# A branch's output projection summed by 64-row halves into separate PSUM banks

## The chip, the cores and the metric

The kernel runs on one core of a Trainium2 chip. A core has a matrix engine (TensorE, PE in the profile; its weight loads are listed as PEld), a vector engine (VectorE, DVE), a scalar engine (ScalarE, ACT), a general engine (GpSimd, POOL) and a queue engine (SyncE, SP) that starts transfers. The matrix engine multiplies a stationary operand (the "weights" of the instruction, here up to 128 rows by 128 columns) with a moving operand and adds the result into an accumulator bank in PSUM; a bank holds 128 partitions by 512 float32. The metric is the device time of one execution in microseconds, lower being better.

## The reference

Two layers, each with one combined input projection, two token mixers and one output projection. The change concerns the line with `w_pa`.

```python
for l in range(DEPTH):                      # DEPTH = 2; x is (1, 256, 1024)
    h = rmsnorm(x, norm_w[l])
    proj = h @ w_in[l]
    q_a, k_a, v_a, ab_a, z_a, q_b, k_b, v_b, z_b, gate_a, gate_b = split(proj)
    y_a = gated_delta_branch(q_a, k_a, v_a, ab_a, z_a, ...)   # (1, 256, 1024)
    y_b = diff_attention_branch(q_b, k_b, v_b, z_b, ...)      # (1, 256, 1024)
    merged = (sigmoid(gate_a) * (y_a @ w_pa[l])
              + sigmoid(gate_b) * (y_b @ w_pb[l]))
    x = x + merged @ w_out[l]
return rmsnorm(x, final_norm_w)
```

Each branch's result is 256 tokens by 1024 channels and is multiplied by a 1024 by 1024 matrix.

## The kernel before, in words

All large products are taken in a float32 format that the matrix engine reads at a rounded precision (`F32R`). To keep the accuracy, each operand is split into a high part and the remainder, the low part, and a product is summed from three terms: activation high by weight high, activation high by weight low, and activation low by weight high.

A token-major projection (`proj_tm`, lines 315 to 332) makes 512 output columns for all 256 tokens. It has one accumulator bank for each of the two token tiles (m = 0 and 1, 128 tokens each), taken by `banks2` from the pool `ps_p` of four banks. Its loop runs over the eight contraction tiles kt of 128 rows, over the two token tiles, and over the three terms (lines 324, 325 and 326). The activation is stationary, 128 rows by 128 tokens; the weight tile, 128 rows by 512 columns, moves. At the end `evac` is called for each token tile.

The weights come from `weights` (line 273 on), for two contraction tiles at a time: a load of 512 KB on SP's queue into `raw` (line 304), a cast on ACT to the high part (line 308), and a subtraction on DVE to the low part (line 310). The pools of high and low parts have two buffers each, so the cast for one pair of tiles waits until the matrix engine has finished with the pair two steps earlier.

The function `branch` (line 1213 on) calls `proj_tm` twice for a branch, once for each half i of the 1024 output columns, and its `evac_p` (line 1217) multiplies the sum, read from PSUM by DVE, with the gate. The b branch's projection (`pb`) comes before the a branch's (`pa`). After `pa`, for each column half and token tile, DVE adds the two branches (line 1286), and `split_T` turns the sum with four transposes on the matrix engine into a bank of the pool `ps_m` (line 227), copies the high part on ACT (line 234) and subtracts for the low part on DVE (line 238). The result, `mT`, is the activation of the output projection (`o`), whose first half is again a `proj_tm` and whose second half is `proj_by_tile` (line 369, and 359 for the last tile in two column halves).

The pool `ps_c` has two banks. Near this place it serves the last steps of the a branch's recurrence (`chunks(0)`, during `pb`) and later the transposes of the next layer's normalised input (`prenorm`).

Each engine works through its own queue in order. The order within a queue is set when the program is built, by a planner that estimates when each instruction could run and prefers those with higher priority (the weights' loads, casts and subtractions run under `tc.high_priority`). Some instructions are tied to others by `behind`; in `branch` and in `proj_tm` none are.

The attention scores (`scores`, line 1061) are the other place that matters here: for each head and query tile they take one product on rows 64 to 127 and one on rows 0 to 63 of the same tiles, in plain float32, into two banks.

Of the kernel before, what the change touches and what calls it, by code (L numbers as in the profile page):

```python
# [8 lines left out]
F32 = mybir.dt.float32  # L9
# [3 lines left out]
ALU = mybir.AluOpType  # L13
# [4 lines left out]
P = 128  # L18
DM = 1024
KT = DM // P  # L20
SEQ = 256
NM = SEQ // P
# [27 lines left out]
def hybrid_encoder(  # L50
# [19 lines left out]
    V, S, G, T = nc.vector, nc.scalar, nc.gpsimd, nc.tensor  # L70

    def pool(name, bufs=1, space=None):
        kw = {} if space is None else {"space": space}
        return ctx.enter_context(tc.tile_pool(name=name, bufs=bufs, **kw))
# [4 lines left out]
    work = pool("work", 2)  # L79
# [9 lines left out]
    def banks2(name):  # L89
        return [ps_p.tile([P, 512], F32, tag="p", name=f"{name}{i}") for i in range(2)]  # L90

    def banks2_c(name):
        return [ps_c.tile([P, 512], F32, tag="c", name=f"{name}{i}") for i in range(2)]
# [10 lines left out]
    mark = {}  # L104
# [210 lines left out]
    def proj_tm(act, w, c0, n, evac, nm, places=(None,) * 4, spare=(), later=None, turned=(), between=None,  # L315
                banks=None, held=None, first=(), raws={}):

        accs = (banks or banks2)(f"pp_{nm}")
        for kt, hi, lo in weights(w, c0, n, nm, places, later=later, spare=spare, turned=turned, held=held,
                                  first=first, raws=raws):  # L320
            for m in range(NM):
                ts_ = slice(m * P, (m + 1) * P)
                o = accs[m][:, :n]
                T.matmul(o, act[kt // 4][:, 0, kt % 4, ts_], hi, start=kt == 0, stop=False)  # L324
                T.matmul(o, act[kt // 4][:, 0, kt % 4, ts_], lo, start=False, stop=False)  # L325
                mark["proj"] = T.matmul(o, act[kt // 4][:, 1, kt % 4, ts_], hi, start=False,  # L326
                                        stop=kt == KT - 1).ins
                mark["done", nm, kt] = mark["proj"]
        if between:
            between()  # L330
        for m in range(NM):
            evac(m, accs[m][:, :n])

    def homes(tags, nm):

        for tag, n in tags:
            t_ = big.tile([P, n, 2, 2, 512], F32R, tag=tag, name=f"w{tag}_{nm}")
            for k in range(n):
                yield t_[:, k]
# [34 lines left out]
    def proj_fm(act, w, c0, evac, nm, turned=()):  # L374
# [15 lines left out]
                         skip_group_check=True)  # L390
        for i in range(2):
            evac(accs[i], 2 * i)

    halves = (slice(0, 64), slice(64, P))

    def silu2(dst, ps):

# [109 lines left out]
    for l in range(DEPTH):  # L507
# [6 lines left out]
        def evac_v(i):  # L514
            def evac(m, ps):
                S.copy(vb[i][:, m, :], ps)
            return evac


        places = list(homes((("A", 1), ("ktm", 1), ("vtm", 1), ("B", 2)), f"vb{l}"))  # L520

        places2 = pair(f"wvb{l}")
        places2 = [t_.rearrange("p x b t -> p x (b t)").rearrange("p x (k c) -> p x k c", k=2)
                   for t_ in places2] + [places.pop(), *homes((("vtm", 1),), f"vb{l}1")]
        if l == 0:
            opening(wl, evac_v(0), places)
# [101 lines left out]
        for kt in range(KT):  # L628
            for part in range(2):
                T.matmul(abp[0:64, :SEQ], wabr[:, kt, :], hT[kt // 4][:, part, kt % 4, :],  # L630
                         start=kt == 0 and part == 0, stop=kt == KT - 1 and part == 1)
# [3 lines left out]
        for m in range(NM):  # L635
            T.matmul(abq[:, m * 32 : (m + 1) * 32], abT[:, m * P : (m + 1) * P], id2,
                     start=True, stop=True)
# [575 lines left out]
        def branch(yT, w_, gt, nm, places=(None,) * 4):  # L1213
            for i in range(2):
                def evac_p(m, ps, i=i):
                    gs = gt[i][:, m, :]
                    V.scalar_tensor_tensor(gs, gs, 1.0, ps, ALU.add, ALU.mult)
                proj_tm(yT, w_, 512 * i, 512, evac_p, f"{nm}{i}", (None,) * 4 if i else places)

        rgb = big.tile([P, 2, 2, 512], F32, tag="p8", name=f"rgb{l}", bufs=4)  # L1220
# [24 lines left out]
        for i, m in ((0, 0), (0, 1), (1, 0), (1, 1)):  # L1245
            split_B(ybT[i], yb_sent[i, m][0], m, nw[:, 1:2], mark[f"ga{l}{i}", 2 + m])
        branch(ybT, w_pb[l], gtb, f"pb{l}")
        ch = [chunks(0), chunks(1)]

# [22 lines left out]
        for m in range(NM):  # L1272
# [5 lines left out]
            V.scalar_tensor_tensor(ro[:, m], ro[:, m], 0.5, rq[:, m], ALU.mult, ALU.mult)  # L1278
            gated(osb, za, ro, nw[:, 0:1], yaT, f"ya{l}", (m,))
        branch(yaT, w_pa[l], gta, f"pa{l}")  # L1280


# [10 lines left out]
        def evac_o(i):  # L1293
            def evac(m, ps, cs=slice(0, 512)):
# [3 lines left out]

        proj_tm(mT, w_out[l], 0, 512, evac_o(0), f"o{l}0",
                [None, None] + list(homes((("ktm", 1), ("vtm", 1)), f"o{l}0")), spare=(2, 3),  # L1300
                later={2: mark[f"pa{l}0", 3], 3: mark[f"pa{l}1", 1]},
                held={2: mark["load", f"pb{l}1", 1], 3: mark["load", f"pb{l}1", 3]})
# [9 lines left out]
        for m in range(NM if not more else 0):  # L1312
            outs.append(norm_tiles("nf", m))
            h, r, ss = outs[m]
# [5 lines left out]
        for s_, _ in enumerate(o_last):  # L1320
            if more:
                prenorm(s_, xt, wb, l + 1)
            else:

                m = min(s_, 1)
                h, r, ss = outs[m]
# [5 lines left out]
                else:  # L1332
                    cs = slice(256 * (s_ - 1), 256 * s_)
                    part = ss[:, 1:2] if s_ == 1 else small.tile([P, 1], F32, tag="xsl", name="xsl", bufs=1)
# [49 lines left out]
```

## Time and profile before

| what | value |
|---|---|
| median of two runs | 750.91 us (750.02 to 751.8) |
| span of the profiled execution | 748.5 us |
| what lies between that span and the median | 2.4 us |
| TensorE busy | 739.3 us, 99% |
| TensorE weight loads busy | 641.7 us, 86% |
| DVE busy | 586.5 us, 78% |
| ACT busy | 481.2 us, 64% |
| granted TensorE clock, mean | 0.998 |

The page of the profile gives the busy time of each engine, the chain of waits that ended last, and groups of instructions by source line. A row of a tile or line view gives the number of instructions and their shortest, median and longest duration in ns; `128*128 128x512` is the size of the stationary operand and the moving one. A row of the timeline gives the start in us, the time from the first start to the last end of the merged instructions, the engine, the line, the operation, output and inputs, and how many were merged. Products of the matrix engine overlap, so the step from one start to the next says more than a duration. What an idle engine waited for stands in brackets at the end.

### The profile page before, as it was taken

What the parts mean: (1) busy time and instruction counts of PE and PEld (TensorE: products, weight loads), DVE (VectorE), ACT (ScalarE), POOL (GpSimd) and SP (SyncE); (2) the same over time, 40 slices, a digit from 0 to 9 for tenths busy, and PEclk for the clock granted to TensorE, in tenths of its full rate; (3) what the DMA queues carried; (4) which work ended last, traced back from release to release, by engine and by line L of the source; (5) the groups of instructions that cost most, each with busy time, mean ns of one, the idle gap of its engine ahead of it and who ended that gap; (6) DMA issues with size and microseconds to landing.
All of it is one profiled execution on the core that took longest, in us unless ns stands there. A gap on an engine that the chain in (4) does not pass through costs nothing.

```text
span 748.5 us, 13917 instructions
## 1 busy us (share of the span) xinstructions
PE 739.3 (99%) x5176; PEld 641.7 (86%) x5176; DVE 586.5 (78%) x1109; ACT 481.2 (64%) x1022; POOL 139.5 (19%) x221
## 2 busy tenths in 40 slices
PE   8999999999999999999999999999999999999996
PEld 6999889987888889888889899889778888998885
DVE  8696898999985965578668779999999679537782
ACT  6757875667876576645456578555687757566552
POOL 6004110112023440100000150202110425301000
PEclk9999999999999999999999999999999999999999
DMA  8754566776667462567674466767666748335641
GB/s 260 239 170 169 170 179 198 209 211 193 208 177 186 145 184 84 171 200 247 199 232 133 128 192 180 219 176 230 195 171 195 197 133 229 95 114 201 220 141 57
DMA packets 73734, 135.46 MB, mean 181 GB/s; under 512 B 12944, under 2 KB 13921, under 8 KB 73666
## 3 DMA queue, kind: packets, MB, share of 16 engines
q1 hardware_dynamic: 64750, 113.65, 50.6%
q0 software_dynamic: 7936, 19.35, 8.7%
q10 hardware_dynamic: 980, 1.58, 0.6%
q8 instruction: 41, 0.67, 0.4%
q14 instruction: 27, 0.22, 0.1%
HBM read 125.53 MB, written 9.01 MB: 180 GB/s over the span
## 4 chain that ended last, share of the span: by engine, by line
PE 95%; ACT 2%; issue 1%; DVE 1%; DMA 1%; SPq 0%; POOLq 0%; POOL 0%; DVEq 0%; ACTq 0%
PE pp_vb L369 4%; PE pp_qk L325 4%; PE pp_qk L326 3%; PE pp_qk L324 3%; PE sc L1061 2%; PE pp_o L369 2%; PE pf_k L385 2%; PE pp_za L325 2%; PE pf_v L385 2%; PE pf_v L389 2%; PE pp_gb L324 2%; PE pp_gb L325 2%; PE pp_zb L324 2%; PE pf_q L387 2%; PE pf_k L387 2%; PE pf_v L387 2%
## 5 line engine op out<-in xcount | busy, mean ns | idle before, releaser
L325 PE MATMUL pp_qk<-lo_qk,hT 128*128 128x512 f32 x128 | 50.5, 395 | 0.3
L326 PE MATMUL pp_qk<-hi_qk,hT 128*128 128x512 f32 x128 | 50.0, 390 | 0.0
L310 DVE TENSOR_TENSOR lo_qk<-raw_qk,hi_qk 128x1024 fp32r<-128x1024 f32 x32 | 39.1, 1222 | 11.6 <-ACT hi_qk L308 11.4
L324 PE MATMUL pp_qk<-hi_qk,hT 128*128 128x512 f32 x128 | 45.1, 393 | 0.0
L308 ACT CAST hi_qk<-raw_qk 128x1024 fp32r<-128x1024 f32 x28 | 29.4, 1049 | 23.4 <-PE pp_qk L326 12.4
L1071 ACT ACTIVATE es<-sc,mx 128x256 f32<-128x256 f32 x64 | 29.6, 474 | 19.5 <-DVE mx L1069 19.5
L387 PE MATMUL pf_q<-hT,hi_q 128*128 128x256 f32 x128 | 36.1, 286 | 0.0
L385 PE MATMUL pf_k<-hT,hi_k 128*128 128x256 f32 x128 | 36.1, 287 | 0.0
L385 PE MATMUL pf_v<-hT,hi_v 128*128 128x256 f32 x128 | 35.9, 285 | 0.0
L387 PE MATMUL pf_v<-hT,hi_v 128*128 128x256 f32 x128 | 35.8, 284 | 0.0
L385 PE MATMUL pf_q<-hT,hi_q 128*128 128x256 f32 x128 | 35.8, 284 | 0.0
L387 PE MATMUL pf_k<-hT,hi_k 128*128 128x256 f32 x128 | 35.8, 284 | 0.0
L310 DVE TENSOR_TENSOR lo_pb<-raw_pb,hi_pb 128x1024 fp32r<-128x1024 f32 x16 | 19.6, 1225 | 20.5 <-ACT hi_pb L308 20.2
L389 PE MATMUL pf_q<-hT,lo_q 128*128 128x256 f32 x128 | 35.2, 288 | 0.0
L389 PE MATMUL pf_v<-hT,lo_v 128*128 128x256 f32 x128 | 34.6, 288 | 0.0
L389 PE MATMUL pf_k<-hT,lo_k 128*128 128x256 f32 x128 | 34.3, 284 | 0.0
L308 ACT CAST hi_pa<-raw_pa 128x1024 fp32r<-128x1024 f32 x16 | 16.8, 1053 | 22.3 <-PE pp_pa L326 16.1
L679 DVE SCALAR_TENSOR_TENSOR cvq<-pf_q,cw,cvq 128x254 f32<-128x254 f32 (+1 forms) x64 | 30.0, 479 | 0.9 <-ACT cvq L675 0.3
L679 DVE SCALAR_TENSOR_TENSOR cvv<-pf_v,cw,cvv 128x254 f32<-128x254 f32 (+1 forms) x64 | 30.1, 482 | 0.1
L679 DVE SCALAR_TENSOR_TENSOR cvk<-pf_k,cw,cvk 128x254 f32<-128x254 f32 (+1 forms) x64 | 29.0, 478 | 1.3 <-ACT cvk L675 0.6
L325 PEld LDWEIGHTS pp_qk<-lo_qk,hT 128*128 128x128 f32 x128 | 24.0, 188 | 6.6 <-DVE lo_qk L310 1.6
L310 DVE TENSOR_TENSOR lo_pa<-raw_pa,hi_pa 128x1024 fp32r<-128x1024 f32 x16 | 19.6, 1224 | 11.1 <-ACT hi_pa L308 11.1
(414 smaller groups left out, 2542.2 us busy)
## 6 DMA issues: line engine op xcount, KB each, us to landing
raw_qk<-in_w_in_dram SPq DMA_DIRECT2D x32, 512.0 KB, 3.8
raw_k<-in_w_in_dram SPq DMA_DIRECT2D x16, 512.0 KB, 4.7
raw_q<-in_w_in_dram SPq DMA_DIRECT2D x16, 512.0 KB, 3.7
raw_v<-in_w_in_dram SPq DMA_DIRECT2D x16, 512.0 KB, 3.8
raw_zb<-in_w_in_dram SPq DMA_DIRECT2D x16, 512.0 KB, 3.7
raw_za<-in_w_in_dram SPq DMA_DIRECT2D x16, 512.0 KB, 3.7
raw_ga<-in_w_in_dram SPq DMA_DIRECT2D x16, 512.0 KB, 4.4
raw_pb<-in_w_pb_dram SPq DMA_DIRECT2D x16, 512.0 KB, 3.8
```

The lines of the kernel that those rows point to most:

```text
L308: high = (V.tensor_copy if kp in turned else S.copy)(hi[:, :, :n], raw[:, :, :n]).ins
L310: mark[nm, kp] = high, V.tensor_tensor(lo[:, :, :n], raw[:, :, :n], hi[:, :, :n].bitcast(F32), ALU.subtract).ins
L324: T.matmul(o, act[kt // 4][:, 0, kt % 4, ts_], hi, start=kt == 0, stop=False)
L325: T.matmul(o, act[kt // 4][:, 0, kt % 4, ts_], lo, start=False, stop=False)
L326: mark["proj"] = T.matmul(o, act[kt // 4][:, 1, kt % 4, ts_], hi, start=False, stop=kt == KT - 1).ins
L369: mark["proj"] = T.matmul(o, act[kt // 4][:, pa, kt % 4, ts_], ws[kt][1 + pw], start=kt == 0 and n_ == 0, stop=kt == KT - 1 and n_ == 2).ins
L385: T.matmul(o, hi[:, cs], act[kt // 4][:, 0, kt % 4, :], start=first, stop=False, skip_group_check=True)
L387: T.matmul(o, hi[:, cs], act[kt // 4][:, 1, kt % 4, :], start=False, stop=False, skip_group_check=True)
L389: T.matmul(o, lo[:, cs], act[kt // 4][:, 0, kt % 4, :], start=False, stop=done, skip_group_check=True)
L679: V.scalar_tensor_tensor(ca[:, o0:o1], acc[:, b, o0 + sft : o1 + sft], cw[:, j, cb : cb + 1], ca[:, o0:o1], ALU.mult, ALU.add)
L1061: mm = T.matmul(sp[n][:, qt * SEQ : (qt + 1) * SEQ], qkT[h // 4][rows, 0, h % 4, qt * P : (qt + 1) * P], qkT[h // 4][rows, 1, h % 4, :], s ...
L1071: S.activation(es[:, n, qt, :], spv[:, qt, :], AF.Exp, bias=mx[:, n, qt : qt + 1], accum_out=s_all[:, h, n, qt : qt + 1])
```

## The change

The projection of the a branch no longer goes through `proj_tm` but through a new function. Every product of 128 contraction rows is replaced by two products, one on rows 0 to 63 and one on rows 64 to 127 of the same operands. The lower rows are summed into two banks of `ps_p` as before, the upper rows into two banks of `ps_c`. When both are complete, ACT copies the one sum to a tile in SBUF, DVE adds the other to it, and the evacuation reads that tile instead of PSUM. The loads, casts and subtractions of the weights are the same. The tuple `halves` is defined earlier in the file, unchanged.

```diff
+    halves = (slice(0, 64), slice(64, P))
+
+    def proj_rows(act, w, c0, evac, nm):
+        accs = [banks2(f"pp_{nm}"), banks2_c(f"pu_{nm}")]
+        for kt, hi, lo in weights(w, c0, 512, nm):
+            for m in range(NM):
+                for n_, (part, w_) in enumerate(((0, hi), (0, lo), (1, hi))):
+                    for r in range(2):
+                        mark["proj"] = T.matmul(accs[r][m], act[kt // 4][halves[r], part, kt % 4, m * P : m * P + P],
+                                                w_[halves[r]], start=kt == 0 and n_ == 0,
+                                                stop=kt == KT - 1 and n_ == 2).ins
+        for m in range(NM):
+            both = work.tile([P, 512], F32, tag="w2c", name=f"sum_{nm}{m}", bufs=3)
+            S.copy(both, accs[0][m])
+            V.tensor_tensor(both, accs[1][m], both, ALU.add)
+            evac(m, both)
...
                 def evac_p(m, ps, i=i):
                     gs = gt[i][:, m, :]
                     V.scalar_tensor_tensor(gs, gs, 1.0, ps, ALU.add, ALU.mult)
+                if nm[:2] == "pa":
+                    proj_rows(yT, w_, 512 * i, evac_p, f"{nm}{i}")
+                    continue
                 proj_tm(yT, w_, 512 * i, 512, evac_p, f"{nm}{i}", (None,) * 4 if i else places)
```

More of the change, by code (lines that the diff above doesn't have):

```diff
@@ L392, in proj_fm @@
             evac(accs[i], 2 * i)
-    halves = (slice(0, 64), slice(64, P))
     def silu2(dst, ps):
```

## The prediction, made before the changed kernel ran

> **What bounds the kernel now.** The page comes first, for the engine that carries the span.
>
> ```profile
> span 748.5 us, 13917 instructions
> ...
> PE 739.3 (99%) x5176; PEld 641.7 (86%) x5176; DVE 586.5 (78%) x1109; ACT 481.2 (64%) x1022; POOL 139.5 (19%) x221
> ...
> PEclk9999999999999999999999999999999999999999
> ...
> PE 95%; ACT 2%; issue 1%; DVE 1%; DMA 1%; SPq 0%; POOLq 0%; POOL 0%; DVEq 0%; ACTq 0%
> ```
>
> TensorE (PE) is busy for 99% of the span and makes up 95% of the chain of waits; its granted clock shows no throttling in any slice. So whatever the edit adds to the PE queue, as work or as a wait, is added to the time, and whatever it adds to ACT (64% busy) or DVE (78%) costs only where PE then waits for it. The profiled execution has a span of 748.5 us against a median of 750.91: about 2.4 us lie around the span or between executions. I work out a difference from this one execution and add it to the median.
>
> The tile view of the accumulators that the edit replaces says how much work is concerned.
>
> ```profile
> L324 PE MATMUL pp_pa<-hi_pa,yaT x64: 389/389/393, 330.0 to 718.0; 128*128 128x512 f32 x64
> ...
> L325 PE MATMUL pp_pa<-lo_pa,yaT x64: 389/389/476, 330.5 to 718.2; 128*128 128x512 f32 x64
> ...
> L326 PE MATMUL pp_pa<-hi_pa,yaT x64: 389/389/395, 330.7 to 718.4; 128*128 128x512 f32 x64
> L1217 DVE SCALAR_TENSOR_TENSOR ga<-ga,pp_pa x8: 680/680/683, 340.6 to 719.0; 128x512 f32<-128x512 f32 x8
> ```
>
> There are 192 products over both layers (two layers, two column halves, eight contraction tiles, two token tiles, three terms) and 8 evacuations. The durations of 389 ns are latencies; products overlap, so the price of one is the step between starts. That needs the timeline, here at the seam between the first column half (pa0) and the second (pa1) of layer 0.
>
> ```profile
> 340.00 0.39 PE L326 MATMUL pp_pa<-hi_pa,yaT 128*128 128x512 f32 x1
> ...
> 340.23 0.39 PE L324 MATMUL pp_pa<-hi_pa,yaT 128*128 128x512 f32 x1
> 340.23 0.19 PEld L325 LDWEIGHTS pp_pa<-lo_pa,yaT 128*128 128x128 f32 x1
> ...
> 340.62 1.28 DVE L1217 SCALAR_TENSOR_TENSOR ga<-ga,pp_pa 128x512 f32<-128x512 f32 x2
> 340.68 0.39 PE L326 MATMUL pp_pa<-hi_pa,yaT 128*128 128x512 f32 x1
> ...
> 340.91 0.61 PE L324 MATMUL pp_pa<-hi_pa,yaT 128*128 128x512 f32 x2
> 341.11 1.06 ACT L308 CAST hi_pa<-raw_pa 128x1024 fp32r<-128x1024 f32 x1 [1.67 <-PE pp_pa L326]
> ...
> 344.09 1.03 PE L227 MATMUL pt_mg<-ident,ga 128*128 128x128 f32 x8
> ```
>
> Products start every 0.227 us (340.68 to 340.91), each with the next one's weights loading beside it (the load that starts at 340.23 together with a product). PE goes from pa0 to pa1 without a gap, because pa1 uses two other banks of the pool of four.
>
> **The split products: do two halves cost one whole?** Each 128-row product becomes two 64-row products, one on the lower and one on the upper rows. The nearest rows are the attention scores, which already alternate the two row halves; the windows are cut so that the pairs show.
>
> ```profile
> L1061 PE MATMUL sc<-qkT x128: 376/376/481, 165.0 to 591.0; 64*128 64x256 f32 x128
> ...
> 164.65 0.39 PE L326 MATMUL pp_zb<-hi_zb,hT 128*128 128x512 f32 x1
> ...
> 164.97 0.70 PE L1061 MATMUL sc<-qkT 64*128 64x256 f32 x4
> ...
> 165.28 0.38 PE L1061 MATMUL sc<-qkT 64*128 64x256 f32 x2
> ...
> 165.29 0.19 PEld L1061 LDWEIGHTS sc<-qkT 64*128 64x128 f32 x2
> ...
> 165.50 0.60 PE L1061 MATMUL sc<-qkT 64*128 64x256 f32 x4
> ...
> 165.72 0.38 PE L1061 MATMUL sc<-qkT 64*128 64x256 f32 x2
> ...
> 166.03 0.66 PE L608 MATMUL qkt<-ident,stg 128*128 128x128 f32 x4
> ...
> 192.42 1.14 PE L1061 MATMUL sc<-qkT 64*128 64x256 f32 x8
> 193.48 0.50 PE L325 MATMUL pp_za<-lo_za,hT 128*128 128x512 f32 x1
> 193.82 0.39 PE L326 MATMUL pp_za<-hi_za,hT 128*128 128x512 f32 x1
> ```
>
> At 165.72 two products together take 0.38 us, while one alone has a duration of 376 ns: they run side by side. So do their weight loads (165.29: two in 0.19). Pairs start every 0.22 us (165.28, 165.50, 165.72). So the new 192 pairs should cost about what 192 products cost now, 0.22 to 0.227 us each.
>
> Which one? The scores are plain float32, which streams 256 columns in about the time that the projection's format streams 512. Two rows of the projection's own format show what lies on top of the streaming.
>
> ```profile
> 735.90 1.60 PE L359 MATMUL pp_o<-wkq_o,mT 128*128 128x256 f32 x12
> ...
> 22.63 1.99 PE L630 MATMUL abp<-hT,wabr 128*64 128x256 f32 x16
> L630 PE MATMUL abp<-hT,wabr x32: 276/277/355, 22.6 to 390.6; 128*64 128x256 f32 x32
> ```
>
> With 128 weight columns the step for 256 columns is (1.60-0.28)/11 = 0.120 us (the last one's latency taken from the last row); twice the columns give 0.227, so a column costs 0.107/256 us and 0.013 us are constant. With 64 weight columns the step is (1.99-0.28)/15 = 0.114, a constant of 0.007. The constant goes with the number of weight columns loaded, and each half still loads 128. I therefore take 0.227 for a pair: 0 us. The ends are 0.22 (the scores), 192 x -0.007 = -1.3 us, and the constant paid twice, 192 x 0.013 = +2.5 us. The Trainium skill (TensorEngine Tiling (Array Packing), Performance Considerations, When to Use Tiling) recommends row tiling where the contraction is at most 64; here it is 128 and fills the array. By that rule the rate gains nothing, by the scores' row it gains the 1.3 us; no row here has this format with 64 rows.
>
> **Switching between 128 and 64 rows.** From the last whole product at 164.65 to the first pair at 164.97 is 0.32 instead of 0.227, and from there to the second pair (165.28) 0.31 instead of 0.22: the weight load is exposed once. In: 0.09+0.09 = 0.18 us. Out: the eight scores from 192.42 end at 193.56, so the last pair began at 193.18; the next whole product comes 0.30 later instead of 0.22, and the one after that 0.34 later (193.48 to 193.82) instead of 0.227: 0.19 us. Into transposes (165.72 to 166.03, 0.31) the visible part is 0.09. Per layer the new stretch is entered after the b branch's projection, left and re-entered at the transposes at 344.09, and left into the output projection: 2 x 0.18 + 0.19 + 0.09 and a little for the transposes' own load, about 0.7 us; two layers +1.4 us.
>
> **The wait at the seam.** The new second accumulators lie in a pool of two banks, so pa1's upper-row products cannot begin until pa0's sums are read. Prices of the two new instructions, from groups with the same operands:
>
> ```profile
> L597 ACT COPY stg<-pp_qk 128x512 f32<-128x512 f32 x16 | 9.3, 579 | 2.4 <-PE pp_qk L326 2.3
> L1027 DVE TENSOR_TENSOR kq<-po,kq 128x512 f32<-128x512 f32 x8 | 5.5, 687 | 7.2 <-PE po L1025 7.2
> ```
>
> Token tile 0 ends with the product at 340.00+0.39 = 340.39; copy to 340.97, add to 341.66, while pa1 could start at 340.91: PE waits 0.75 us, 0.85 with an estimated 0.1 for the hand-overs. Token tile 1 ends at 341.07; its copy competes with the cast of 341.11 (1.06 us), its add with tile 0's evacuation (0.68) and a low-part subtraction (1.22, quoted below). With add directly behind add there is no more wait after three pairs of tile 0 (0.68 us); with the evacuation between, 0.65 more; with the subtraction too, 1.9 more. So 0.85, 1.5 or 2.7 us per seam. I take 1.5, the order of the program text; it is +3.0 us for two layers (1.7 to 5.4). If the planner lets the lower-row products run ahead alone, each then needs its partner alone later: the same price. Behind the waiting product in PE's queue stand all of pa1, the transposes and the output projection.
>
> **The end of pa1.** The merged gate needs the sums later too.
>
> ```profile
> 351.77 0.39 PE L326 MATMUL pp_pa<-hi_pa,yaT 128*128 128x512 f32 x1
> ...
> 352.38 1.28 DVE L1217 SCALAR_TENSOR_TENSOR ga<-ga,pp_pa 128x512 f32<-128x512 f32 x2
> ...
> 353.58 1.29 DVE L1286 TENSOR_TENSOR ga<-ga,gb 128x512 f32<-128x512 f32 x2
> 354.78 1.22 DVE L310 TENSOR_TENSOR lo_o<-raw_o,hi_o 128x1024 fp32r<-128x1024 f32 x1
> 355.86 1.04 PE L227 MATMUL pt_mg<-ident,ga 128*128 128x128 f32 x8
> 356.65 0.47 PE L325 MATMUL pp_o<-lo_o,mT 128*128 128x512 f32 x1
> ```
>
> Today tile 0 is complete at 352.16, DVE runs two evacuations and two additions, then a subtraction that ends at 356.00; PE uses it at 356.65, so 0.65 us are spare. Afterwards DVE starts at 352.16+0.6 = 352.78 and has six operations of 0.6 us step instead of four: 356.4, and the subtraction to 357.6, so PE would wait 1.0 us. If the subtraction goes first it is hidden and the transposes come at 356.4 instead of 355.86, a wait of 0.55. Range 0 to 1.4, value 0.8 per layer, +1.6 us. The same chain after pa0 has its cover in the seam's wait, which moves the transposes back by as much. Copies (8 x 0.58 us ACT) and additions (8 x 0.69 us DVE) cost nothing elsewhere: the first run while ACT waits 1.67 us for PE before the cast. Loads keep their number and order: nothing.
>
> **Sum.** 0 + 1.4 + 3.0 + 1.6 = +6.0 us: span 754.5, time 750.9 + 6.0 = 756.9. Low end -1.3+1.4+1.7+0 = +1.8 (752.7); high end 2.5+1.4+5.4+2.8 = +12.1 (763.0).
>
> **Rivals.**
> *The halves do not run side by side* (the change does not do what it says; slower). Each half then takes its own 0.22 us: 192 x (2 x 0.22 - 0.227) = +40.9, with 6.0 for the rest 797.8. It leaves the 2% once a pair takes (15.0-6.0)/192 = 0.047 us more than a whole product. For it: no row has this format in halves. Against: products and loads of the scores are side by side. Chance 0.07.
> *The planner separates the pairs.* Instructions are ordered by an estimate; if halves are issued apart for two weight tiles per layer (24 pairs, as far as the double-buffered weights reach), each costs an extra 0.22: 2 x 24 x 0.22 = 10.6 in place of the seam's 3.0: 764.5, and more if it reaches further. For it: nothing ties the halves together, and the waiting bank makes one half ready earlier. Chance 0.10.
> *Pairs at 0.22 and most waits covered*: the low end, 752.7, or a little less; for it speaks that the planner may put the additions first, against it that the two-bank pool leaves at least the copy and one addition uncovered. Chance 0.12.
> *Weight loads were exposed and are now hidden* (faster). If a whole product could not have its weights loaded beside the one before, a pair, on other rows, could: the exposed load is 0.09 us (165.28-164.97-0.22), 192 x -0.09 = -17.3, with the +6.0 739.6; to end below 735.9 the load would have to be larger than the one seen. The Trainium skill (TensorE: Matmul & The Clock Gate, Part 3, The mechanism) says loads overlap running products only on other row groups. By that rule this rival would hold; the trace disagrees, since the load at 340.23 starts with a running product on the same rows and the step stays 0.227. Chance 0.02.
> The forecast keeps 0.69.
>
> **Range and chances.** 751.5 to 765 leaves out the first and last rivals, about half of the planner's tail (0.05) and a little below the low end (0.04): 0.18 in all. The measurement tells about 2% (15 us) from no change. Slower, above 766: 0.07 plus 0.04 of the planner's case, 0.11. Faster, below 735.9: 0.02, all of the last rival, whose price sits near that edge. Within: 0.87.
>
> **What will show it.** In the changed kernel: 384 products 64*128 on the new line, two per 0.22 to 0.23 us; a gap of PE, or a run of lone halves, of 0.85 to 2.7 us at the start of pa1, put down to the DVE addition; 0.3 us steps at the switches; a wait of up to 1.4 us at the low parts in the output projection. Steps of 0.43 us per pair, or halves far apart, would make the prediction wrong upwards; pairs at 0.22 with no wait at the seam, downwards.

## The result, and the profile after

The changed kernel takes 762.72 us (762.71 to 762.73) against 750.91 us: a ratio of 1.0163, 95% interval 1.0127 to 1.0198. That is slower by 11.8 us and inside the 2% that the measurement counts as no change. The forecast was +6.0 us. The direction, the range and the list of places were right; the size is twice the forecast, and most of the missing half lies at one place.

The page of the changed kernel, and the tile view of the new operations (a row: count, shortest/median/longest in ns, first and last start):

```profile
span 761.0 us, 14317 instructions
...
PE 94%; ACT 2%; DVE 2%; issue 1%; POOLq 0%; POOL 0%; DVEq 0%; ACTq 0%
...
L343 PE MATMUL pp_pa<-hi_pa,yaT x128: 383/387/497, 330.2 to 728.5; 64*128 64x512 f32 x128
...
L348 ACT COPY sum_pa<-pp_pa x8: 586/586/587, 340.8 to 729.0; 128x512 f32<-128x512 f32 x8
L349 DVE TENSOR_TENSOR sum_pa<-pu_pa,sum_pa x8: 683/688/692, 341.4 to 730.2; 128x512 f32<-128x512 f32 x8
```

The 192 more products, 8 copies and 8 additions are there. PE still makes up 94% of the chain of waits, so the page doesn't say where 12.5 us of span went. Starts of products do. Two stages hold it all: the a branch's projection (first `pa` product to first `o` product) and the first half of the output projection (from there to the first product of its second half).

| stage | before, layers 0 and 1 | after, layers 0 and 1 | difference, both layers |
|---|---|---|---|
| `pa` | 22.65 and 22.65 us | 25.59 and 25.59 | +5.9, and +0.2 for the step into it |
| first half of `o` | 11.81 and 11.81 | 16.07 and 14.38 | +6.8 |
| everything else | | | -0.4 |

The timeline of PE around the seam from `pa0` to `pa1`, layer 0:

```profile
341.05 0.39 PE L343 MATMUL pp_pa<-hi_pa,yaT 64*128 64x512 f32 x1
341.06 0.38 PE L343 MATMUL pu_pa<-hi_pa,yaT 64*128 64x512 f32 x1
341.28 0.61 PE L343 MATMUL pp_pa<-hi_pa,yaT 64*128 64x512 f32 x2
...
343.10 0.49 PE L343 MATMUL pu_pa<-hi_pa,yaT 64*128 64x512 f32 x1
...
346.51 0.66 PE L227 MATMUL pt_mg<-ident,ga 128*128 128x128 f32 x4
...
352.79 0.44 PE L227 MATMUL pt_mg<-ident,ga 128*128 128x128 f32 x2
```

The reader is to see three things. A lower (`pp`) and an upper (`pu`) half start within 0.01 us of each other and a pair follows after 0.22 to 0.23 us (341.05 to 341.28): a pair costs what a whole product cost. From 341.28 to 343.10 lower halves run alone, and their partners run alone afterwards: the 14 pairs of this stretch take from 341.28 to 346.42, 5.14 us instead of 14 x 0.227 = 3.18. And the eight transposes, which before stood together at 344.09, come as four (346.51), two (352.79) and two more, below.

The lone lower halves are not explained by the wait that the prediction expected. DVE's addition of the first sum begins at 341.42 and has freed the first upper bank at about 342.11, but the first upper product of `pa1` comes at 343.10:

```profile
341.42 0.69 DVE L349 TENSOR_TENSOR sum_pa<-pu_pa,sum_pa 128x512 f32<-128x512 f32 x1 [0.34 <-ACT sum_pa L348]
```

The end of `pa1`, PE, DVE and ACT of the same layer:

```profile
355.33 0.38 PE L343 MATMUL pu_pa<-hi_pa,yaT 64*128 64x512 f32 x1
355.64 0.44 PE L227 MATMUL pt_mg<-ident,ga 128*128 128x128 f32 x2
355.84 0.48 PE L324 MATMUL pp_o<-hi_o,mT 128*128 128x512 f32 x1
...
357.64 0.50 PE L324 MATMUL pp_o<-hi_o,mT 128*128 128x512 f32 x1 [0.16 <-ACT hi_o L308]
358.45 0.63 PE L227 MATMUL pt_mg<-ident,ga 128*128 128x128 f32 x4 [0.31 <-DVE ga L1305]
360.43 0.50 PE L325 MATMUL pp_o<-lo_o,mT 128*128 128x512 f32 x1 [1.35 <-DVE lo_o L310]
...
361.26 0.63 PE L325 MATMUL pp_o<-lo_o,mT 128*128 128x512 f32 x1
361.69 0.63 PE L326 MATMUL pp_o<-hi_o,mT 128*128 128x512 f32 x1
```

```profile
357.62 0.68 DVE L1305 TENSOR_TENSOR ga<-ga,gb 128x512 f32<-128x512 f32 x1
358.22 0.42 DVE L642 TENSOR_TENSOR wabr<-wab,wabr 128x256 fp32r<-128x256 f32 x1
358.56 0.68 DVE L1233 SCALAR_TENSOR_TENSOR ga<-ga,sum_pa 128x512 f32<-128x512 f32 x1
359.16 1.22 DVE L310 TENSOR_TENSOR lo_o<-raw_o,hi_o 128x1024 fp32r<-128x1024 f32 x1
```

```profile
355.07 1.26 ACT L348 COPY sum_pa<-pp_pa 128x512 f32<-128x512 f32 x2 [1.58 <-PE pu_pa L343]
...
356.54 1.05 ACT L308 CAST hi_o<-raw_o 128x1024 fp32r<-128x1024 f32 x1
```

PE comes to the low part of the second pair of weight tiles at about 359.1 and waits 1.35 us, until 360.43. Its cast on ACT stood behind two copies of sums and ended at 356.54 + 1.05 = 357.59; its subtraction on DVE then stood behind the addition of the two branches, another subtraction and an evacuation of a sum, until 359.16. Before, the same subtraction was ready 0.65 us ahead of its use. After the wait, products take 0.63 us and start 0.43 us apart. The trace has the granted clock change at 361.18 and back at 364.59, 3.41 us later. The stretch before this, the stretch itself and two stretches of the same length at the same place of layer 1 (columns: stretch, length, busy time of PE, PEld, DVE, ACT and POOL with their instructions, granted clock, DMA share, GB/s):

```profile
357.77:361.18 3.41, 1.74 (x8) 1.14 (x9) 3.41 (x5) 2.68 (x4) 0.00 (x0) 1.00 0.07 29
361.18:364.59 3.41, 3.41 (x12) 2.64 (x11) 2.13 (x4) 0.51 (x1) 0.00 (x0) 0.50 0.86 262
729.82:733.23 3.41, 1.85 (x9) 0.98 (x7) 3.41 (x6) 3.41 (x5) 0.00 (x0) 1.00 0.32 115
733.23:736.64 3.41, 3.33 (x16) 2.52 (x17) 2.96 (x5) 0.42 (x2) 0.00 (x0) 1.00 0.00 0
```

In layer 0 the granted clock falls to 0.50 for 3.41 us, which is worth about 3.41 x (1 - 0.50) = 1.7 us; the stage is 1.69 us longer there than in layer 1, where the clock holds.

### The profile page after: what moved, and what is told of

Its sections match the earlier page's. It is cut to its first block, busy times and chain, and to the rows that moved or that the text cites. A ratio compares the mean times of both kernels' runs of the same rounds, so it can differ in the third digit from the quotient of the medians.

```text
span 761.0 us, 14317 instructions
## 1 busy us (share of the span) xinstructions
PE 749.2 (98%) x5368; PEld 645.4 (85%) x5368; DVE 591.8 (78%) x1117; ACT 485.7 (64%) x1030; POOL 139.7 (18%) x221
## 4 chain that ended last, share of the span: by engine, by line
PE 94%; ACT 2%; DVE 2%; issue 1%; POOLq 0%; POOL 0%; DVEq 0%; ACTq 0%
PE pp_pa L343 6%; PE pp_vb L387 4%; PE pp_qk L325 3%; PE pp_qk L326 3%; PE pp_qk L324 3%; PE sc L1077 2%; PE pp_o L387 2%; PE pf_k L403 2%; PE pf_v L403 2%; PE pp_za L325 2%; PE pf_v L407 2%; PE pp_gb L325 2%; PE pp_gb L324 2%; PE pp_zb L324 2%; PE pf_q L405 2%; PE pf_k L407 2%
## 5 line engine op out<-in xcount | busy, mean ns | idle before, releaser
L343 PE MATMUL pu_pa<-hi_pa,yaT 64*128 64x512 f32 x128 | 40.5, 391 | 0.0
L343 PE MATMUL pp_pa<-hi_pa,yaT 64*128 64x512 f32 x128 | 40.5, 391 | 0.0
```

The source lines that it names most:

```text
L343: mark["proj"] = T.matmul(accs[r][m], act[kt // 4][halves[r], part, kt % 4, m * P : m * P + P], w_[halves[r]], start=kt == 0 and n_ == 0, ...
```

## The experiments

Four theories for the 11.8 us stood against each other. *Sums*: the copies and additions come between other work of ACT and DVE and make the low part late. *Order*: each product is now two instructions, and the planner lays out PE's queue differently (lone halves, scattered transposes). *Seam*: the upper sums have only two banks, so `pa1` waits for the reads of `pa0`. *Pairs*: a pair costs more than a whole product, or needs its halves next to each other. The ratios are against the kernel before on the same chip, which stood at 750.1 to 750.4 us. Where the intervals of two runs overlap, as those of e1 or e6 and the changed kernel do, the difference is read from the stages of one profiled execution of each, and not from the medians. In the recorded expectations theory A puts the time into the queues around the sums, theory B into the half-row products themselves, and rival C into the seam.

| run | median us | ratio (95%) | `pa`, layers 0/1 | first half of `o`, layers 0/1 |
|---|---|---|---|---|
| before (profile) | 750.91 | | 22.65/22.65 | 11.81/11.81 |
| after (profile) | 762.72 | 1.0163 (1.0127 to 1.0198) | 25.59/25.59 | 16.07/14.38 |
| e1_no_sum | 759.31 | 1.0120 (1.0105 to 1.0135) | 25.96/25.96 | 13.08/13.07 |
| e2_two_banks | 754.33 | 1.0054 (1.0038 to 1.0071) | 22.65/22.69 | 14.97/12.78 |
| e3_second_half | 754.94 | 1.0063 (1.0048 to 1.0078) | 23.78/23.78 | 13.81/12.79 |
| e4_first_half | 753.25 | 1.0045 (1.0030 to 1.0060) | 24.23/23.91 | 11.77/11.77 |
| e5_home | 773.09 | 1.0298 (1.0283 to 1.0313) | 31.73/32.87 | 14.18/12.90 |
| e6_early_turns | 758.89 | 1.0118 (1.0101 to 1.0135) | 25.61/25.61 | 13.72/12.78 |
| e7_home_turns_tied | 772.99 | 1.0299 (1.0283 to 1.0314) | 32.34/32.66 | 13.97/12.66 |
| e8_apart | 762.26 | 1.0157 (1.0141 to 1.0172) | 26.50/26.54 | 15.09/12.60 |
| e9_low_first | 760.42 | 1.0124 (1.0107 to 1.0141) | 25.61/25.61 | 13.87/12.72 |
| e10_low_first_tied | 759.05 | 1.0114 (1.0092 to 1.0135) | 25.29/25.29 | 13.84/12.74 |
| e11_no_seam | 759.21 | 1.0107 (1.0090 to 1.0124) | 24.48/24.48 | 14.64/12.76 |
| e12_apart_12 | 778.48 | 1.0372 (1.0356 to 1.0387) | 35.10/35.15 | 14.40/12.52 |

### e1_no_sum: halves without the sums

The evacuation reads the lower rows' bank directly, so the result lacks the upper rows' part.

```diff
-            both = work.tile([P, 512], F32, tag="w2c", name=f"sum_{nm}{m}", bufs=3)
-            S.copy(both, accs[0][m])
-            V.tensor_tensor(both, accs[1][m], both, ALU.add)
-            evac(m, both)
+            evac(m, accs[0][m])
```

> The change with the copy and the addition left out: the lower rows' sum alone is evacuated from its bank as before, the upper rows' products run but are not used (the output lacks them). Theory A (the time went into the queues around the evacuation: the seam between the column halves 3.9 us, the low parts in the output projection 6.8 us, and 2.1 us of switching): no seam, no wait at the output projection, only switches, 0.2 us into the stretch, 0.34 us for each group of transposes inside it, 0.15 us out, so 1.2 to 1.4 us per layer: 753.5 us. Theory B (products on half the rows are slower or delay the rest by themselves): most of the 11.8 us stays, 758 us or more.

The ratio falls by 0.43% only, some 3.2 us, where theory A expected 753.5 us. PE's timeline of this run:

```profile
340.97 0.61 PE L343 MATMUL pp_pa<-hi_pa,yaT 64*128 64x512 f32 x2
...
342.79 0.49 PE L343 MATMUL pu_pa<-hi_pa,yaT 64*128 64x512 f32 x1
...
346.20 0.55 PE L227 MATMUL pt_mg<-ident,ga 128*128 128x128 f32 x3
...
359.06 0.50 PE L325 MATMUL pp_o<-lo_o,mT 128*128 128x512 f32 x1 [0.86 <-DVE lo_o L310]
```

Nothing ever reads the upper banks here, and still lower halves run alone from 340.97 until the first upper one at 342.79. The upper halves pause for 2.04 us, as long as in the changed kernel (341.06 to 343.10). The lone halves of the seam are therefore the order of PE's queue, not a wait. The transposes are scattered here too (3, 1, 2 and 2), and the low part is waited for with no sum on DVE: order alone costs 1.27 us per layer in the output projection. So neither theory A as it was put nor theory B holds: the time stays without the sums, though a pair costs no more than a whole product.

### e2_two_banks: the sums without halves

Whole products; even contraction tiles sum into the one bank, odd ones into the other; copies and additions stay.

```diff
-                    for r in range(2):
-                        mark["proj"] = T.matmul(accs[r][m], act[kt // 4][halves[r], part, kt % 4, m * P : m * P + P],
-                                                w_[halves[r]], start=kt == 0 and n_ == 0,
-                                                stop=kt == KT - 1 and n_ == 2).ins
+                    mark["proj"] = T.matmul(accs[kt % 2][m], act[kt // 4][:, part, kt % 4, m * P : m * P + P],
+                                            w_, start=kt < 2 and n_ == 0,
+                                            stop=kt >= KT - 2 and n_ == 2).ins
```

> Whole 128-row products, but the even contraction tiles summed into one pair of banks and the odd ones into the other, with the same copy, addition and evacuation. Theory A: no switches; the seam is covered, because six whole products on the first tile (1.36 us) need only the free banks; at the output projection the low part still stands behind two additions and two evacuations on DVE and its cast behind two copies on ACT, a wait of about 1 to 1.5 us per layer: 753 to 754 us. Theory B: no half-row products, so the time of before, 751 us.

The projection takes its old 22.65 us, in one unbroken run of products. In the output projection the waits of layer 0 are:

```profile
356.89 0.50 PE L325 MATMUL pp_o<-lo_o,mT 128*128 128x512 f32 x1 [0.50 <-DVE lo_o L310]
361.97 0.50 PE L324 MATMUL pp_o<-wktm_o,mT 128*128 128x512 f32 x1 [1.63 <-ACT mT L234]
```

Layer 1 grows by 12.78 - 11.81 = 0.97 us. That is the price of the sums at the end of `pa1` when PE has the same 14 products ahead of the low part as before; the prediction had 0.8. The order is not the old one throughout: the eight transposes now follow behind the low part (359.30, where they stood ahead of it at 355.86), and about half of the 0.97 us lies at the low part, the other half between the transposes and the products that need them. Layer 0 adds the second row: the cast of the transposed gate (`mT`) is late on ACT. The median is just above the 753 to 754 us of theory A, and theory B's 751 is ruled out.

### e3_second_half and e4_first_half: one column half at a time

```diff
-                if nm[:2] == "pa":
+                if nm[:2] == "pa" and i == 1:     # e3; e4 has i == 0
```

> Only the second column half of the a branch's projection is split by rows; the first goes as before. Theory A: no wait at the seam, as the two-bank pool is free; the output projection waits as in the changed kernel (2.6 to 4.3 us per layer, the larger with the clock drop); switches about 0.8 us per layer: 757.5 to 759.5 us. Rival C (the seam is the main cost): 752.5 us.

> Only the first column half is split by rows; the second goes as before. Theory A: no seam (the second half uses two other banks), the output projection waits for an evacuation as in the kernel before, so only one entry and one exit per layer, 0.4 us each layer: 751.8 us. Theory B: half of the rise, about 757 us. Rival C says 752 us too; together with the run on the second half it leaves for the seam what neither has.

Both medians miss what was expected: e3 lies between theory A's 757.5 and rival C's 752.5 us, e4 1.4 us above the 751.8 that both gave. With `pa0` alone in halves (e4) the output projection keeps its time (11.77): its excess belongs to the sums and the order at the end of `pa1`. With `pa1` alone in halves (e3) it is again 12.79 in layer 1, and a wait for `lo_o` is back (0.9 us in layer 0, 0.5 in layer 1). Neither has the seam, since neither uses the upper banks twice in a row, and their ratios add to 1.08%, some 8.1 of the 11.8 us. Stage by stage this sum doesn't close (3.0 of 6.8 us in the output projection), so it is no proof for the seam's size. In e4 the whole products of `pa1` wait 0.86 us for a low part of `pa1`'s own weights, so its 1.3 to 1.6 us per layer are not switches alone.

### e6_early_turns: the first column half's transposes early

```diff
             for m in range(NM):
-                V.tensor_tensor(gta[i][:, m, :], gta[i][:, m, :], gtb[i][:, m, :], ALU.add)
-                split_T(mT[i], heads4(gta[i][:, m, :]), m, f"mg{l}{i}")
+                with tc.high_priority(offset=HP) if i == 0 else nullcontext():
+                    V.tensor_tensor(gta[i][:, m, :], gta[i][:, m, :], gtb[i][:, m, :], ALU.add)
+                    split_T(mT[i], heads4(gta[i][:, m, :]), m, f"mg{l}{i}")
```

> The change, with the gated sum, transposes and split of the first column half given priority, so that they are not put off to the end of the second half. Theory A: 14 products instead of 7 stand ahead of the late low part, whose lateness on DVE stays; a wait of 1 to 1.5 us per layer remains in the output projection, and no drop of the clock: 758 to 759.5 us. Rival (the low part alone sets the wait, wherever the transposes are): 762 us.

```profile
355.57 0.73 PE L324 MATMUL pp_o<-hi_o,mT 128*128 128x512 f32 x2
...
358.45 0.62 PE L324 MATMUL pp_o<-hi_o,mT 128*128 128x512 f32 x2
...
360.36 0.50 PE L325 MATMUL pp_o<-lo_o,mT 128*128 128x512 f32 x1 [0.84 <-DVE lo_o L310]
```

With all of the first half's gate turned before the output projection begins, PE has 14 products to do ahead of the late low part (355.57 to 358.45) where the changed kernel had seven, and reaches it later. The stage falls from 16.07 and 14.38 to 13.72 and 12.78: 3.95 us, the scatter and the lost clock that followed from it; the median is within the 758 to 759.5 expected. What is left in layer 1 is 0.97 us, as much as in e2. Layer 0 keeps 0.94 us more: a small subtraction for the next layer makes the low part later still, and the cast of `mT` stands behind a cast that waits for a transfer.

### e5_home and e7_home_turns_tied: a place of its own for the second weights

```diff
-                [None, None] + list(homes((("ktm", 1), ("vtm", 1)), f"o{l}0")), spare=(2, 3),
+                [None] + list(homes((("A", 1), ("ktm", 1), ("vtm", 1)), f"o{l}0")), spare=(2, 3),
```

e7 has e6's edit as well, and ties the halves to the order of the program text.

> The change, with one pair of weight tiles of the output projection's first half (the second pair, whose low part DVE delivers late) put into the free tile A instead of the double-buffered pool, so that its cast and subtraction need not wait for the end of the a branch's projection. Theory A (order in the queues): the wait for the low part goes, 24 products stand ahead of the transposes, and the output projection's first half falls from 16.1 and 14.4 us to about 12: 756 to 757 us. Theory B (half-row products themselves): unchanged, 762 to 763 us.

> Both of these, and the half-row products tied to their program order, so that no lower half runs ahead at the seam. Theory A: what is left is the seam as a wait (0.85 to 1.5 us per layer instead of 2.0) and the switches (1.0 us per layer): 754 to 756 us. Theory B: 762 us.

These were meant to take the low part out of the two-buffer pool, and became tests of something else. ACT's queue in e5:

```profile
353.85 1.04 ACT L308 CAST wA_o<-raw_o 128x1024 fp32r<-128x1024 f32 x1 [5.85 <-DMA raw_o<-in_w_out_dram]
...
355.75 1.04 ACT L308 CAST hi_pa<-raw_pa 128x1024 fp32r<-128x1024 f32 x1
```

The casts of the output projection's weights now stand ahead of the last cast of `pa1`, and the first of them waits 5.85 us for its transfer. PE waits for `hi_pa` in its turn, and `pa` takes 32 us. The medians are 773 us in place of the 754 to 757 expected, and on the low part both are inconclusive.

### e9_low_first and e10_low_first_tied: the low part ahead of the sums

On top of e6, the output projection's first weights are written before `pa1`'s evacuation, and the second token tile's sum and the second column half's addition of the branches wait for them (the main lines of the edit). e10 also ties the halves in program order.

```diff
+        if between:
+            between()
         for m in range(NM):
             both = work.tile([P, 512], F32, tag="w2c", name=f"sum_{nm}{m}", bufs=3)
-            S.copy(both, accs[0][m])
-            V.tensor_tensor(both, accs[1][m], both, ALU.add)
-            evac(m, both)
+            cast, low = mark[f"o{nm[2]}0", 1] if between and m else (None, None)
+            with behind(cast):
+                S.copy(both, accs[0][m])
+            with behind(low):
+                V.tensor_tensor(both, accs[1][m], both, ALU.add)
+                evac(m, both)
...
+                    with behind(None if i == 0 else mark[f"o{l}0", 1][1]):
+                        V.tensor_tensor(gta[i][:, m, :], gta[i][:, m, :], gtb[i][:, m, :], ALU.add)
```

> The change with the early transposes of the run before, and in the second column half the evacuation of the second token tile tied behind the late cast and low part of the output projection's weights (no other tile, no other load). Theory A (order on DVE and ACT): the low part is ready before it is used, 24 products stand ahead of the transposes, the output projection's first half takes 11.8 to 12.3 us; left are the seam (2.0 us per layer) and the switches (1.0 us): 756 to 757 us. If the wait has another cause, it stays at the 758.9 of the run with early transposes alone.

> The same, with the half-row products tied to their program order, so that no lower half runs ahead at the seam. Theory A: the seam becomes a plain wait for the two additions, 0.65 and 0.5 us and one exposed weight load, 1.4 instead of 2.0 us per layer: 755 to 756 us. If lone halves and the wait cost the same, as the prediction had it: 756 to 757 us.

Both miss the time expected, 755 to 757 us. In the profiled execution of e9, 1.9 us are lost before `pa` even begins (331.83 against 329.96 in e6), in a part that the edit doesn't touch. The wait for `lo_o` is gone, and others take its place. PE and ACT of e9, layer 0:

```profile
364.05 0.63 PE L227 MATMUL pt_mg<-ident,ga 128*128 128x128 f32 x4 [0.41 <-DVE ga L1321]
365.26 0.50 PE L324 MATMUL pp_o<-wktm_o,mT 128*128 128x512 f32 x1 [0.58 <-ACT mT L234]
```

```profile
363.68 1.05 ACT L308 CAST wA_vb<-raw_vb 128x1024 fp32r<-128x1024 f32 x1 [2.39 <-DMA raw_vb<-in_w_in_dram]
364.63 1.07 ACT L234 CAST mT<-pt_mg 128x512 fp32r<-128x512 f32 x2
```

If the sums go last, the second half's gate is late instead, and the stage stays at 12.72 to 12.74 in layer 1. So the 0.9 to 1.0 us per layer is not the place of one instruction: DVE and ACT have two more operations each in this stretch, and in each of the orders tried (e2, e6, e9) PE waits for what stands last. In layer 0 the cast of `mT` stands behind the cast of the next layer's weights, which waits 2.39 us for its transfer; layer 1 has no next layer, and its stage is 1.15 us shorter.

e10 shows the seam as the prediction described it, because the halves stay together:

```profile
341.37 0.39 PE L344 MATMUL pp_pa<-hi_pa,yaT 64*128 64x512 f32 x1
342.25 0.50 PE L344 MATMUL pu_pa<-hi_pa,yaT 64*128 64x512 f32 x1 [0.49 <-DVE sum_pa L356]
342.58 0.39 PE L344 MATMUL pu_pa<-lo_pa,yaT 64*128 64x512 f32 x1
...
342.82 0.39 PE L344 MATMUL pp_pa<-hi_pa,yaT 64*128 64x512 f32 x1
343.57 0.49 PE L344 MATMUL pu_pa<-hi_pa,yaT 64*128 64x512 f32 x1 [0.36 <-DVE sum_pa L356]
```

Two stops, both put down to the addition. The steps 341.37 to 342.25 and 342.82 to 343.57, and one of 0.34 behind each, are 1.4 us longer than four steps of 0.227. As a whole `pa` is 0.32 us per layer shorter than with the planner's order.

### e11_no_seam: other banks for `pa1`'s upper rows

e9, with `pa1`'s upper sums in the banks of `ps_m` and the transposes in those of `ps_c`.

```diff
-        accs = [banks2(f"pp_{nm}"), banks2_c(f"pu_{nm}")]
+        accs = [banks2(f"pp_{nm}"), [bank(f"pu_{nm}{i}") for i in range(2)] if between else banks2_c(f"pu_{nm}")]
...
-                split_T(mT[i], heads4(gta[i][:, m, :]), m, f"mg{l}{i}")
+                    split_T(mT[i], heads4(gta[i][:, m, :]), m, f"mg{l}{i}", bank_c)
```

> The same as the run with early transposes and low part first, but the second column half's upper sums lie in the two banks that the transposes use, and the transposes use the pool of the first half's upper sums, so that no product waits for a sum. Theory A: no seam; the low part of the second half's weights, which stands behind the evacuations on DVE, now loses its cover and costs about 0.5 us per layer; with the switches (1.0 us) 753.5 to 755 us, of which the half-row products as such have only the switches.

`pa` falls by 1.13 us per layer against e9, less than the seam's 1.97, in part because a wait that the seam had covered comes up:

```profile
345.80 0.50 PE L343 MATMUL pp_pa<-lo_pa,yaT 64*128 64x512 f32 x1 [0.62 <-DVE lo_pa L310]
```

The median is 1.2 us below e9's, and the two ratios' intervals overlap; the 753.5 to 755 us expected are missed.

### e8_apart and e12_apart_12: halves issued apart

For each weight tile all six lower products, then all six upper ones (e8); for each pair of tiles twelve and twelve (e12), tied in this order. The edit of e8:

```diff
-            for m in range(NM):
-                for n_, (part, w_) in enumerate(((0, hi), (0, lo), (1, hi))):
-                    for r in range(2):
-                        mark["proj"] = T.matmul(...)
+            for r in range(2):
+                for m in range(NM):
+                    for n_, (part, w_) in enumerate(((0, hi), (0, lo), (1, hi))):
+                        with behind(mark["tie"] if kt + m + n_ + r else None):
+                            mark["tie"] = mark["proj"] = T.matmul(...)
```

> The change, with the halves kept apart: for each contraction tile six products on the lower rows, then six on the upper rows, in that order. If products start strictly in the order of the queue, only one product in six meets its partner: 5 more steps of 0.227 us for each of 32 contraction tiles, +36 us, about 798 us. If each half of the rows works through its own products and the queue looks ahead over some of the other half's, much of that is regained: 765 to 785 us.

> The change with twelve products on the lower rows, then twelve on the upper rows, for each pair of weight tiles. The run with blocks of six took no longer than the change. If the queue looks ahead without limit for the other half of the rows: again about 762 us. If it looks ahead by six products or so, about half of each block is alone: 16 blocks x 6 x 0.227 us, +22 us, about 784 us. With strict order 16 x 11 x 0.227, +40 us, about 802 us.

Blocks of six cost 0.9 us per layer in `pa` over the changed kernel, which has lone halves of its own at the seam, and 1.2 over e10, where the halves stay in pairs; blocks of twelve cost 9.5 over the changed kernel. For e8 765 us or more was expected, for e12 762, 784 or 802. PE of e12 (`pp` lower, `pu` upper):

```profile
334.62 0.39 PE L348 MATMUL pu_pa<-hi_pa,yaT 64*128 64x512 f32 x1
334.63 0.49 PE L348 MATMUL pp_pa<-hi_pa,yaT 64*128 64x512 f32 x1
334.85 0.39 PE L348 MATMUL pu_pa<-hi_pa,yaT 64*128 64x512 f32 x1
334.96 0.39 PE L348 MATMUL pp_pa<-lo_pa,yaT 64*128 64x512 f32 x1
335.07 0.39 PE L348 MATMUL pu_pa<-lo_pa,yaT 64*128 64x512 f32 x1
...
335.30 0.39 PE L348 MATMUL pu_pa<-hi_pa,yaT 64*128 64x512 f32 x1
...
338.54 0.49 PE L348 MATMUL pp_pa<-hi_pa,yaT 64*128 64x512 f32 x1
```

The next lower block starts at 334.63, 0.01 us behind one upper product (334.62) and ahead of three more that the ties put before it in the queue (334.85, 335.07, 335.30). The two row halves are two streams, and one may run ahead of the queue's order by about four products. Blocks of six then overlap almost wholly. Of twelve, four overlap at each end and four run alone, each in a step that could have carried a pair: with 16 blocks per layer that is 16 x 4 / 2 = 32 steps too many, 7.3 us, plus a step of about 0.11 at the start of each (334.63 to 334.96 in `pp`), 1.8: 9.1 in all. The trace has 3.91 us from one lower block to the next (334.63 to 338.54), 1.19 more than twelve steps of 0.227, and eight such stretches per layer come to 9.5.

## Why the prediction was right or wrong, point by point

| term, both layers | predicted us | measured us |
|---|---|---|
| pairs for whole products | 0 | 0 |
| switches of row mode | 1.4 | 2.1 |
| seam | 3.0 | 3.9 |
| end of `pa1` and the output projection | 1.6 | 6.8 |
| else | 0 | -0.4 |
| sum (span) | 6.0 | 12.5 |

**Pairs: right.** Starts are together and the step stays at 0.22 to 0.23 us; the constant is not paid twice and not saved. By the recommendation of the Trainium skill (TensorEngine Tiling (Array Packing), Performance Considerations, When to Use Tiling), row tiling is for contractions of at most 64. Taken as a rule it gives no gain in rate at 128, and the trace agrees, 0 us. The rival that halves don't run side by side falls by the same rows. So does the rival of exposed weight loads: if loads had been hidden for the first time, the step would be shorter.

**Switches: right in kind, short by a third.** What `pa` lost beyond the seam is 3.03 - 1.97 = 1.06 us per layer, where 0.7 was forecast. The price of one switch was about right (355.33 to 355.64 is 0.31 instead of 0.22); the count was not. The prediction left and re-entered the 64-row mode once for eight transposes, and the planner made three groups of them.

**Seam: right place, 2.0 instead of 1.5 us per layer, by another mechanism.** In the changed kernel it isn't the wait for the addition: that addition (341.42, 0.69 us) had freed the first upper bank at about 342.11, the first upper product came at 343.10, and the pause is the same 2.04 us in e1, where nothing reads that bank. It is twelve lower halves queued ahead of their twelve partners. With the overlap of four that e12 shows, eight run alone on each side: 8 x 0.227 = 1.8 us more than pairs, and the rest of 1.97 in the longer steps at the joins. The prediction named this form and called it the same price, which holds to 0.3 us a layer (`pa` in e9 and in e10). The wait itself, where ties keep the halves together (e10), is 1.4 us against the 1.5 taken.

**The end of `pa1`: the step that failed.** It said that the low part of the output projection would be 1.0 us late or the transposes 0.55, and took 0.8 per layer. With 14 products ahead of the low part, as before, that is nearly right in size: 0.97 us in layer 1 of e2, and 0.97 again in e6. (A small slip in its working, 352.16 + 0.6 taken as 352.78, changes nothing.) What failed is the premise behind it, that PE would come to that low part with the same work ahead of it. The planner spread the first half's transposes over `pa1`, the last two just ahead of the output projection, and PE then had seven products instead of 14 to run before the late low part. That cost 14.38 - 12.78 = 1.60 us in layer 1, so a layer loses 0.97 + 1.60 = 2.57; order without sums (e1, 1.27) and sums without halves (e2, 0.97) add to nearly that. Layer 0 lost 1.69 more, where the idle time was followed by 3.41 us at a clock of 0.50, worth 1.7. So 6.8 = 2 x 2.57 + 1.69. The late `mT` of layer 0 in e2 and e6 has no part in this: the changed kernel's PE doesn't wait for it.

**The rival of separated pairs** gave 764.5 us, near the result, but not by its working. The order did change, for 12 pairs per layer; but it priced each separated pair at an extra 0.22 us, 21 us per layer if all 96 were apart. e8 separates all by six and pays 0.9 over the changed kernel, e12 all by twelve and pays 9.5.

**Copies and additions elsewhere: right.** `pa` without them (e1) is 25.96 us, no shorter than with them.

No version here beat the kernel before. The lowest with halves in both column halves are e6, e10 and e11, at 758.89 to 759.21 us (ratios 1.0107 to 1.0118), which their intervals don't tell apart. What stays open is why the clock fell in layer 0 and not in layer 1 after nearly the same idle time, and what e6's order would give with the cast of `mT` ahead of the next layer's weights; neither was tried.

## What to carry to other kernels

Where a planner sets the order, cutting instructions into smaller ones is a change of order too: price the terms at the old order, then ask which instruction could be moved and what slack it takes along. A late operand is priced by the work that its reader has ahead of it, and it's that work which should be checked in the new queue, not only the producer's chain. Cutting a 128-row contraction in two saves nothing in rate here, and adds switches, a second set of banks and two operations per sum.

## What the runs showed of the hardware that was not expected

**Row halves run as two streams.** A product on one row half started ahead of up to three products on the other half that stood before it in the queue (e12, 334.63 against 334.85, 335.07 and 335.30). So the sentence of the description that each engine works through its queue in order holds here within a row half, and not across the two. Blocks of six per half cost 0.9 us per layer of 96 pairs over the changed kernel, blocks of twelve 9.5. The Trainium skill (TensorE: Matmul & The Clock Gate, Part 3, The mechanism) says that products start strictly in the order of the queue; these rows disagree for products on different row halves.

**A short idle time took the clock.** 1.67 us of idle PE in a stretch of 3.41 (1.74 busy) was followed by 3.41 us at 0.50; nearly the same idle time in layer 1 (1.85 busy) left the clock at 1.00. The Trainium skill (TensorE: Matmul & The Clock Gate, Part 1, What's actually happening) describes free-running windows of about 3.4 us and a clock that falls after an idle one. The length agrees: the trace has the clock change at 361.18, at 364.59 and, at the end of the kernel, at 757.13, which lie whole steps of 3.413 us apart (1 and 115). An idle window it was not, since PE was busy for half of it.

Counted on in the same steps, 729.82 is such a point too. The idle time of either layer thus lies almost whole within one step, and the phase of the steps doesn't tell the two apart. Nor does the busy time alone: in e12 a step of its own count with 1.71 us busy, first row below, was followed by the full clock. Why one fell and not the other stays open.

```profile
370.87:374.28 3.41, 1.71 (x13) 1.30 (x12) 1.02 (x2) 1.69 (x3) 0.00 (x0) 1.00 0.82 264
374.28:377.69 3.41, 3.26 (x13) 2.29 (x14) 3.41 (x5) 2.22 (x3) 0.00 (x0) 1.00 0.51 137
```
